# Where weights and activations stand modulo 512 bytes: a decoder block on one core

## The chip, the core and the metric

The kernel runs on one core of one Trainium2 chip. The time is the device time of one execution in microseconds (us). TensorE is called PE, its weight loads PEld, VectorE DVE, ScalarE ACT, GpSimd POOL, and the queue that issues the DMAs of weights SP. SBUF is the on-chip memory: 128 partitions, in each of which a tile takes the same range of bytes. "The place" of a tile is the byte in the partition at which it begins, taken modulo 512.

## The reference, cut to what matters

One decoder layer on x of 256 tokens by 2048 channels, in float32:

```python
proj = x @ w_in                         # q, k, v, gates of two mixers, merge gates
o_gla = gated_linear_attention(...) ; o_fox = forgetting_attention(...)
merged = sigmoid(ma) * (o_gla @ w_branch_gla) + sigmoid(mb) * (o_fox @ w_branch_fox)
x = layer_norm(ALPHA * x + merged @ w_out)
h = gelu(causal_dwconv(x @ w_gate)) * (x @ w_up)
x = layer_norm(ALPHA * x + h @ w_down)
x = x + sigmoid(x @ w_ple_gate) * (p @ w_ple_proj)
```

Nearly all of the arithmetic is in the products with weight matrices.

## The kernel before, in words

A product of float32 numbers is made of three products of a shorter format (float32r). Each operand is split into `hi`, its rounded value, and `lo`, the rest: a product is hi·hi + lo·hi + hi·lo, all summed in PSUM. ACT makes `hi` from a raw row (`copy`, line 101), DVE makes `lo` = raw - hi (line 127). Activations are kept split in tiles `xT`, `oT`, `mT`, `x1T`, `hT`, `x2T`: per 128 channels 256 numbers of hi tokens and 256 of lo tokens.

The weights come from HBM in 284 units (`wu`), each of two halves of 128x1024 numbers. `prep` (lines 116 to 130) loads a half into a `raw` tile (4 of them), and ACT and DVE make a `hi` and a `lo` tile of it (6 each). `unit` gives out units in order, up to three ahead. A matmul has two operands in SBUF: the stationary one, 128 columns which PEld loads into the array, and the moving one, which streams through it. There are two kinds of stages:

- **Weights stationary** (`w_unit`, lines 190 and 192; `w_phase`, lines 203 and 207). For each 128x128 block of weights: the hi weights are loaded and 512 columns of activations (hi and lo tokens) stream, then the lo weights are loaded and 256 columns (hi tokens) stream. These are the projections fq, fk, gq, gk (`psfq`, `psfk`, `psq`, `psk`), the merge gates (`psm`), the branches (`psa`, `psb`), and gate and up of the MLP (`psg`, `psu`). `w_phase` makes the first three units of the MLP in two halves of the tokens, each matmul with 256 columns: first all hi weights for one half (line 203), then hi and lo weights in turn (lines 203 and 207).
- **Activations stationary** (`x_mm`, line 234). For each block of 128 tokens, hi tokens are loaded and hi weights stream (512 columns, two banks `c`), then hi tokens and lo weights, then lo tokens and hi weights. These are `gv`, `gr`, `wo`, `dn`, `pg`, and the small projection `pp`, whose weights `pw` are tiles of their own. The first stage, `fv` (line 341), does the same with tiles of 1048 columns in three chunks (`fch`).

The order of the instructions of each engine comes from a list scheduler that works by the program's order and given priorities; SP's DMAs stand in program order. The mixers' small work is pulled in between by generators.

Pools are laid one behind another in SBUF, so the size of each pool sets the places of all behind it. Two pools hold nothing but a gap: `gap0` (64 bytes) between the hi and the lo tiles, and `gap1` (448 bytes) behind the lo tiles. The places (modulo 512 bytes) that come of it:

| tiles | before | after the change |
|---|---|---|
| hi weights, in weights-stationary units | 0 | 64 |
| hi weights, in activations-stationary units | 0 | 0 |
| lo weights | 64 | 0 |
| activations, `pw`, `fvhi`, `fvlo` (pool `big`) | 0 | 0 |
| chunks of `fv` within their tiles | 0, 384, 256 | 0, 0, 0 |
| raw rows of weights (4 tiles) | 0, 96, 192, 288 | 0 |
| `t1`, `t2` (small tiles of mixers and evacuations) | 384 | 0 |
| `hT10` (last hidden block of the MLP) | 128 | 0 |

Within these tiles blocks begin at whole multiples of 512 bytes, so a block's place is that of its tile.

Of the kernel before, what the change touches and what calls it, by code (L numbers as in the profile page):

```python
# [9 lines left out]
F32 = mybir.dt.float32  # L10
F32R = mybir.dt.float32r
# [8 lines left out]
P = 128  # L20
# [6 lines left out]
FH = 8  # L27
# [5 lines left out]
NS = 1048  # L33
# [4 lines left out]
AFF_DVE = (0, 2)  # L38
LN_ORDER = (1, 0, 3, 2)
GROWS = 96  # L40
PAD = 88
S8W = 2048

OFF = dict(gq=0, gk=1024, gv=2048, gr=4096, glr=6144, fq=6160, fk=7184, fv=8208,
           ff=9232, ma=9240, mb=11288)
# [3 lines left out]
def tile_block(ctx: ExitStack, tc: tile.TileContext, wu, wfv, wpp, xT_in, x_in, pT_in, wlr,  # L49
# [1 line left out]
    nc = tc.nc  # L51

    cst = ctx.enter_context(tc.tile_pool(name="cst", bufs=1))
    wide_hi = ctx.enter_context(tc.tile_pool(name="wide_hi", bufs=6))
    step = ctx.enter_context(tc.tile_pool(name="step", bufs=1))
    gap0 = step.tile([P, 16], F32, name="gap0")
    wide_lo = ctx.enter_context(tc.tile_pool(name="wide_lo", bufs=6))
    step2 = ctx.enter_context(tc.tile_pool(name="step2", bufs=1))
    gap1 = step2.tile([P, 112], F32, name="gap1")
    big = ctx.enter_context(tc.tile_pool(name="big", bufs=15))  # L60
    ring = ctx.enter_context(tc.tile_pool(name="ring", bufs=4))
    sm = ctx.enter_context(tc.tile_pool(name="sm", bufs=2))
# [6 lines left out]
    chn = cst.tile([P, chan.shape[1]], F32, name="chn")  # L69
    ident = cst.tile([P, P], F32, name="ident")  # L70
    mhalf = cst.tile([P, 1], F32, name="mhalf")
    pad = cst.tile([P, PAD], F32, name="pad")

    def s8(shape, dt=F32, name=None):
        t = big.tile([P, S8W], dt, tag="S8", name=name)
        n = int(np.prod(shape[1:]))
        t = t[:shape[0], :n]
        if len(shape) == 3:
            return t.rearrange("p (a b) -> p a b", b=shape[2])
        if len(shape) == 4:  # L80
            return t.rearrange("p (a b c) -> p a b c", b=shape[2], c=shape[3])
        return t

    def w_tile(tag, dt, name):
        pool = wide_hi if tag == "hi" else wide_lo
        return pool.tile([P, 1024], dt, tag=tag, name=name)

    def t1(name):
        return sm.tile([P, 256], F32, tag="t1", bufs=6, name=name)

    def t2(name):
        return sm.tile([P, 512], F32, tag="t2", bufs=6, name=name)

    def mmtile(name):
        return pmm.tile([P, 512], F32, tag="mm", name=name)
# [4 lines left out]
    def copy(o, i, scale=1.0):  # L100
        nc.scalar.activation(o, i, AF.Copy, bias=0.0, scale=scale)  # L101
# [15 lines left out]
    def prep():  # L117
        u = n_prep[0]
        n_prep[0] += 1
        his, los = [], []  # L120
        for h in range(2):
            raw = ring.tile([P, 1024], F32, tag="raw", bufs=4, name=f"raw{u}_{h}")
            nc.sync.dma_start(raw, wu[u, :, h * 1024:(h + 1) * 1024])
            hi = w_tile("hi", F32R, f"hi{u}_{h}")
            copy(hi, raw)
            lo = w_tile("lo", F32R, f"lo{u}_{h}")
            nc.vector.tensor_tensor(lo, raw, hi.bitcast(F32), ALU.subtract)  # L127
            his.append(hi)
            los.append(lo)
        ready[u] = (his, los)  # L130
# [4 lines left out]
    def unit():  # L135
        u = n_used[0]
        n_used[0] += 1
        while n_prep[0] < min(NU, u + 3):
            prep()
        return ready.pop(u)  # L140
# [161 lines left out]


    fv = s8([P, 2, 1024], name="fv")
    fch = ((0, 352), (352, 352), (704, 344))
    fbk = [[mmtile(f"fv_{t}{c}") for c in range(3)] for t in range(2)]

    def fv_prep(u, hs=(0, 1), his=None, los=None):
        his, los = his or [], los or []
        for h in hs:  # L310
            raw = ring.tile([P, NS], F32, tag="raw", bufs=4, name=f"fvraw{u}_{h}")
            hi = s8([P, NS], F32R, name=f"fvhi{u}_{h}")
            lo = s8([P, NS], F32R, name=f"fvlo{u}_{h}")
            for o, n in fch if u == 0 else ((0, NS),):
                e = slice(o, o + n)
                nc.sync.dma_start(raw[:, e], wfv[u, :, h, e])
                copy(hi[:, e], raw[:, e])
                nc.vector.tensor_tensor(lo[:, e], raw[:, e], hi[:, e].bitcast(F32), ALU.subtract)
            his.append(hi)
            los.append(lo)  # L320
        return his, los

    load_x(0, 0, 1, 1)
    f0 = fv_prep(0, (0,))
    load_x(0, 1, 2, 1)
    fvu = [fv_prep(0, (1,), *f0)]
    load_x(0, 2, 4)
    fvu.append(fv_prep(1))
    load_x(1, 0, 4)
    for u in range(8):  # L330
        hi, lo = fvu[u]
        for j in range(2):
            kt = 2 * u + j
            a = xT[kt // 4][:, kt % 4, :]
            for cs in ((0,), (1,), (2,)) if u == 0 else ((0, 1, 2),):
                for t in range(2):
                    ah, al = a[:, t * P:t * P + P], a[:, 256 + t * P:256 + t * P + P]
                    for i, (w, x) in enumerate(((hi[j], ah), (lo[j], ah), (hi[j], al))):
                        for c in cs:
                            o, n = fch[c]  # L340
# [20 lines left out]
    for t in range(2):  # L361
        tk = t1("smtok")
        nc.gpsimd.memset(tk, 0.0)
        for i in range(3):
            copy(tk[:, 32 * i:32 * i + 16], fbk[t][2][:, 320:336])
        copy(tk[:, P:P + FH], fbk[t][2][:, 336:344])
        nc.tensor.transpose(smp[:GROWS, t * P:t * P + P], tk[:, 0:GROWS], ident)
        nc.tensor.transpose(smp[:FH, 256 + t * P:256 + t * P + P], tk[:, P:P + FH], ident)
    for t in range(2):
# [147 lines left out]
    for nm, dst, sc in (("fq", fq, P ** -0.5), ("fk", fk, 1.0)):  # L517
        if nm == "fk":
            mixers.append(fox_gen())
        for n in range(8):  # L520
            hi, lo = unit()
# [8 lines left out]
    for nm, dst, sc in (("q", gq, 1.0 / 16.0), ("k", gk, 1.0)):  # L530
        for n in range(8):
            hi, lo = unit()
            ps = mmtile(f"ps{nm}{n}")
            w_unit(ps, hi, lo, xT, range(16), True, True)
            h, c = n // 2, n % 2
# [163 lines left out]
    for n in range(32):  # L699
        hi, lo = unit()  # L700
# [7 lines left out]
        pull(1)  # L708
    early.close()
    late = ctx.enter_context(tc.tile_pool(name="late", bufs=1))  # L710


    mT = [s8([P, 4, 512], F32R, name=f"mT{i}") for i in range(4)]
    fhl = None
    for n in range(16):
        hi, lo = unit()
# [162 lines left out]
        return banks  # L879

    z1 = [s8([P, 2048], name=f"z1{t}") for t in range(2)]
    st1 = [sm.tile([P, 4, 6], F32, tag=f"st1{t}", bufs=1, name=f"st1{t}") for t in range(2)]
    gain = [None, None]

    def mid1():
# [82 lines left out]
    tc.keep_in_program_order(nc.scalar.preload_act_table_set("gelu_apprx_tanh_and_others"))  # L968


    gp = [late.tile([P, 264], F32, name=f"gp{i}") for i in range(2)]
    for i in range(2):
        nc.gpsimd.memset(gp[i][:, 0:2], 0.0)
    hT = [None] * 11
# [12 lines left out]
    for n in range(NF):  # L987
# [17 lines left out]
        u = t1("up")  # L1005
# [6 lines left out]
            pull(1)  # L1012

    z2 = [s8([P, 2048], name=f"z2{t}") for t in range(2)]
    st2 = [sm.tile([P, 4, 6], F32, tag=f"st2{t}", bufs=1, name=f"st2{t}") for t in range(2)]

    def mid2():
        for t in range(2):
# [127 lines left out]
```

## Time and profile before

| what | value |
|---|---|
| median of 3 runs | 1701.79 us (1701.62 to 1701.97) |
| the profiled execution, its own time | 1702.23 us |
| its span, first to last instruction | 1699.5 us |
| granted clock of TensorE | 1.0 |
| PE busy, PEld busy | 99%, 86% of the span |
| DVE, ACT, POOL busy | 65%, 49%, 2% |
| matmuls | 9035 |

What lies around the span is 2.7 us. A matmul's busy time in the profile runs from its first column to a modelled end, and matmuls overlap; so a busy PE says nothing of how fast it goes. What one matmul costs is the time from its start to the next one's start. Where matmuls of one kind follow each other, the mean duration of a row less the overlap with the next gives the same thing.

### The profile page before, as it was taken

The numbers are of one execution on the slowest core, as the hardware profiler recorded it, in microseconds if no ns is written. First come the engines' busy times: TensorE is split into PE (matmuls) and PEld (weight loads), VectorE is DVE, ScalarE is ACT, GpSimd is POOL, SyncE is SP. The second block draws the span as 40 slices with busy tenths as digits, with TensorE's granted clock in tenths as the row PEclk, the third lists the DMA queues.
The fourth block names the chain that finished last, engine by engine and source line by source line (L and its number), as shares of the span: only waits on it lengthen the run. The fifth ranks groups of instructions, "written<-read, shape, count | busy, mean of one in ns | idle before, by whom it ended". The sixth has DMA issues, their size and how long they took to land.

```text
span 1699.5 us, 23843 instructions
## 1 busy us (share of the span) xinstructions
PE 1690.2 (99%) x9035; PEld 1456.4 (86%) x9035; DVE 1098.0 (65%) x1588; ACT 833.9 (49%) x1200; POOL 36.7 (2%) x123
## 2 busy tenths in 40 slices
PE   9999999999999999999999999999999999999998
PEld 8888888888888888888888888888888888888787
DVE  6666658758756547774687776666666644544774
ACT  5655545445555544443365445445445433334633
POOL 0100000000000000000010000000000000000000
PEclk9999999999999999999999999999999999999999
DMA  7765555555555556557656665555555575566455
GB/s 266 260 198 166 165 185 180 178 175 178 181 174 173 162 187 192 190 189 281 220 165 197 215 215 191 192 190 188 188 195 188 191 287 189 187 194 199 158 175 172
DMA packets 91427, 330.22 MB, mean 194 GB/s; under 512 B 10232, under 2 KB 11904, under 8 KB 89904
## 3 DMA queue, kind: packets, MB, share of 16 engines
q1 hardware_dynamic: 90528, 324.51, 58.8%
q0 software_dynamic: 784, 4.20, 0.7%
q8 instruction: 70, 1.15, 0.3%
q14 instruction: 45, 0.37, 0.1%
HBM read 323.42 MB, written 5.25 MB: 193 GB/s over the span
## 4 chain that ended last, share of the span: by engine, by line
PE 98%; DVE 1%; ACT 0%; DMA 0%; SPq 0%; issue 0%; POOL 0%; ACTq 0%
PE dn L234 14%; PE psu L190 9%; PE psg L190 9%; PE psm L190 7%; PE gv L234 5%; PE gr L234 5%; PE pg L234 5%; PE wo L234 5%; PE psu L192 5%; PE psg L192 5%; PE psm L192 4%; PE psa L190 3%; PE fv L341 2%; PE psa L192 2%; PE psq L190 2%; PE psfk L190 2%
## 5 line engine op out<-in xcount | busy, mean ns | idle before, releaser
L127 DVE TENSOR_TENSOR lo<-raw,hi 128x1024 fp32r<-128x1024 f32 x568 | 694.2, 1224 | 506.9 <-ACT hi L101 505.7
L101 ACT ACTIVATE hi<-raw 128x1024 fp32r<-128x1024 f32 x568 | 601.7, 1060 | 732.6 <-issue 274.7
L190 PE MATMUL psu<-x1T,hi 128*128 128x512 f32 x688 | 240.4, 392 | 0.0
L190 PE MATMUL psg<-x1T,hi 128*128 128x512 f32 x672 | 234.8, 392 | 0.0
L192 PE MATMUL psu<-x1T,lo 128*128 128x256 f32 x688 | 192.3, 280 | 0.0
L234 PE MATMUL dn<-hi,hT 128*128 128x512 f32 x704 | 192.1, 392 | 0.0
L192 PE MATMUL psg<-x1T,lo 128*128 128x256 f32 x672 | 187.8, 280 | 0.0
L190 PE MATMUL psm<-xT,hi 128*128 128x512 f32 x512 | 179.8, 395 | 0.0
L234 PEld LDWEIGHTS dn<-hi,hT 128*128 128x128 f32 x704 | 132.1, 188 | 30.6
L190 PEld LDWEIGHTS psu<-x1T,hi 128*128 128x128 f32 x688 | 129.2, 188 | 27.6
L190 PEld LDWEIGHTS psg<-x1T,hi 128*128 128x128 f32 x672 | 126.2, 188 | 27.0
L192 PE MATMUL psm<-xT,lo 128*128 128x256 f32 x512 | 143.2, 280 | 0.0
L192 PEld LDWEIGHTS psu<-x1T,lo 128*128 128x128 f32 x688 | 130.6, 190 | 0.0
L192 PEld LDWEIGHTS psg<-x1T,lo 128*128 128x128 f32 x672 | 127.6, 190 | 0.0
L190 PEld LDWEIGHTS psm<-xT,hi 128*128 128x128 f32 x512 | 96.2, 188 | 21.2
L234 PE MATMUL dn<-lo,hT 128*128 128x512 f32 x352 | 111.9, 395 | 0.0
L192 PEld LDWEIGHTS psm<-xT,lo 128*128 128x128 f32 x512 | 97.0, 189 | 0.2
L190 PE MATMUL psa<-oT,hi 128*128 128x512 f32 x256 | 89.5, 392 | 0.0
L234 PEld LDWEIGHTS dn<-lo,hT 128*128 128x128 f32 x352 | 66.1, 188 | 14.8
L234 PE MATMUL gv<-hi,xT 128*128 128x512 f32 x256 | 72.6, 395 | 0.0
L234 PE MATMUL gr<-hi,xT 128*128 128x512 f32 x256 | 72.4, 395 | 0.0
L192 PE MATMUL psa<-oT,lo 128*128 128x256 f32 x256 | 71.6, 280 | 0.0
(247 smaller groups left out, 2435.2 us busy)
## 6 DMA issues: line engine op xcount, KB each, us to landing
raw<-in_wu_dram SPq DMA_DIRECT2D x568, 512.0 KB, 4.6
fvraw<-in_wfv_dram SPq DMA_DIRECT2D x14, 524.0 KB, 6.5
lnb<-in_lng_dram SPq DMA_DIRECT2D x4, 1024.0 KB, 13.3
z<-in_x_dram SPq DMA_DIRECT2D x2, 1024.0 KB, 9.5
praw<-in_wpp_dram SPq DMA_DIRECT2D x4, 512.0 KB, 4.5
x1d<-z POOLq DMA_DIRECT2D x2, 1024.0 KB, 7.6
z<-x1d SPq DMA_DIRECT2D x2, 1024.0 KB, 9.6
xraw<-in_xT_dram SPq DMA_DIRECT2D x7, 256.0 KB, 7.1
```

Of the source, the lines that this page charges most:

```text
L101: nc.scalar.activation(o, i, AF.Copy, bias=0.0, scale=scale)
L127: nc.vector.tensor_tensor(lo, raw, hi.bitcast(F32), ALU.subtract)
L190: nc.tensor.matmul(ps, lhsT=hi[i // 8 if hoff == 0 else 0][:, w0 % 1024:w0 % 1024 + P], rhs=a[:, kt % 4, :], start=first and i == 0, stop= ...
L192: nc.tensor.matmul(ps[:, 256:512], lhsT=lo[i // 8 if hoff == 0 else 0][:, w0 % 1024:w0 % 1024 + P], rhs=a[:, kt % 4, 0:256], start=False, ...
L234: nc.tensor.matmul(bs[j][:, 0:m], lhsT=x, rhs=v[:, o:o + m], start=first and i == 0, stop=last and i == 2)
L341: nc.tensor.matmul(fbk[t][c][:, 0:n], lhsT=x, rhs=w[:, o:o + n], start=kt == 0 and i == 0, stop=kt == 15 and i == 2)
```

## The change

The hi and lo tiles come out of one pool `wide`. A hi tile is 1152 numbers wide instead of 1024, and its 1024 numbers are put 16 numbers (64 bytes) into it in units whose weights are stationary, and at its beginning in the units of `XSTAT` (gv, gr, wo, dn, pg). The lo tiles, and with them all pools behind, come to 0 modulo 512 bytes. The raw rows of the first stage, 1048 numbers wide, are taken from the six hi tiles instead of the four raw tiles, which so shrink to 1024 numbers. The chunks of `fv` are 384, 384 and 280 columns instead of 352, 352 and 344. `gp`, the two buffers of the MLP's convolution, are two of the six `t2` tiles instead of tiles of the pool `late`; some small statistics tiles (`st1`, `st2`) and paddings are moved so that the places come out even.

```diff
-    wide_hi = ctx.enter_context(tc.tile_pool(name="wide_hi", bufs=6))
-    step = ctx.enter_context(tc.tile_pool(name="step", bufs=1))
-    gap0 = step.tile([P, 16], F32, name="gap0")
-    wide_lo = ctx.enter_context(tc.tile_pool(name="wide_lo", bufs=6))
-    step2 = ctx.enter_context(tc.tile_pool(name="step2", bufs=1))
-    gap1 = step2.tile([P, 112], F32, name="gap1")
+    wide = ctx.enter_context(tc.tile_pool(name="wide", bufs=6))
...
-    def w_tile(tag, dt, name):
-        pool = wide_hi if tag == "hi" else wide_lo
-        return pool.tile([P, 1024], dt, tag=tag, name=name)
+    def w_tile(tag, dt, name, u):
+        if tag == "lo":
+            return wide.tile([P, 1024], dt, tag=tag, name=name)
+        o = 0 if u in XSTAT else HSTEP
+        return wide.tile([P, WH], dt, tag=tag, name=name)[:, o:o + 1024]
...
-    fch = ((0, 352), (352, 352), (704, 344))
+    fch = ((0, 384), (384, 384), (768, 280))
...
-            raw = ring.tile([P, NS], F32, tag="raw", bufs=4, name=f"fvraw{u}_{h}")
+            raw = wide.tile([P, WH], F32, tag="hi", name=f"fvraw{u}_{h}")[:, 0:NS]
...
-    gp = [late.tile([P, 264], F32, name=f"gp{i}") for i in range(2)]
+    gp = [t2(f"gp{i}")[:, 0:264] for i in range(2)]
```

with `XSTAT = (*range(32, 64), *range(120, 136), *range(224, 284))`, `WH = 1152` and `HSTEP = 16`.

The order of PE, DVE, ACT and SP stays what it was, but for the widths in the first stage. On PE, in the steady part of that stage, one block of tokens before (`fv_126` to `fv_131` are its six banks, `fvhi` and `fvlo` the weights, `xT` the tokens):

```order
L341 MATMUL fv_126<-fvhi_0_169,xT_111 128x352
L341 MATMUL fv_127<-fvhi_0_169,xT_111 128x352
L341 MATMUL fv_128<-fvhi_0_169,xT_111 128x344
L341 MATMUL fv_129<-fvhi_0_169,xT_111 128x352
L341 MATMUL fv_130<-fvhi_0_169,xT_111 128x352
L341 MATMUL fv_131<-fvhi_0_169,xT_111 128x344
```

and the same place in the changed program (the numbers of the buffers differ, the banks are the same six):

```order
L344 MATMUL fv_118<-fvhi_0_161,xT_103 128x384
L344 MATMUL fv_119<-fvhi_0_161,xT_103 128x384
L344 MATMUL fv_120<-fvhi_0_161,xT_103 128x280
L344 MATMUL fv_121<-fvhi_0_161,xT_103 128x384
L344 MATMUL fv_122<-fvhi_0_161,xT_103 128x384
L344 MATMUL fv_123<-fvhi_0_161,xT_103 128x280
```

The same matmuls stand in the same order, with the 1048 columns cut elsewhere.

On POOL the two memsets of the borders of `gp` move. Before, they stand ahead of the mixers' second half (`gst`), as soon as the pool `late` is open:

```order
L549 MEMSET at 128x1536
L973 MEMSET gp_8157 128x2
L973 MEMSET gp_8158 128x2
L664 ISA
L664 TENSOR_TENSOR gst<-gst,mhalf 128x1 x8
L786 TENSOR_TENSOR mv<-mv,mhalf 128x1 x2
L910 DMA ppd<-ppo 128x512 x4
L995 COPY gp_8157<-gp_8157 128x1 x2
L995 COPY gp_8158<-gp_8158 128x1 x2
```

In the changed program they stand behind the four DMAs that write `ppo` out, since `gp` now takes `t2` tiles that such work held:

```order
L552 MEMSET at 128x1536
L667 ISA
L667 TENSOR_TENSOR gst<-gst,mhalf 128x1 x8
L790 TENSOR_TENSOR mv<-mv,mhalf 128x1 x2
L913 DMA ppd<-ppo 128x512 x4
L976 MEMSET gp_8148 128x2
L976 MEMSET gp_8149 128x2
L998 COPY gp_8148<-gp_8148 128x1 x2
L998 COPY gp_8149<-gp_8149 128x1 x2
```

The memsets now come right before the first use of `gp` (the copies), 15 instructions later in POOL's order than before.

More of the change, by code (lines that the diff above doesn't have):

```diff
@@ L40 @@
 GROWS = 96
-PAD = 88
+PAD = 16
+LPAD = 24
+XSTAT = (*range(32, 64), *range(120, 136), *range(224, 284))
 S8W = 2048
+WH = 1152
+HSTEP = 16
 OFF = dict(gq=0, gk=1024, gv=2048, gr=4096, glr=6144, fq=6160, fk=7184, fv=8208,
@@ L71, in tile_block @@
     mhalf = cst.tile([P, 1], F32, name="mhalf")
+    st1 = [cst.tile([P, 4, 6], F32, name=f"st1{t}") for t in range(2)]
+    st20 = cst.tile([P, 4, 6], F32, name="st20")
     pad = cst.tile([P, PAD], F32, name="pad")
@@ L123, in prep @@
             nc.sync.dma_start(raw, wu[u, :, h * 1024:(h + 1) * 1024])
-            hi = w_tile("hi", F32R, f"hi{u}_{h}")
+            hi = w_tile("hi", F32R, f"hi{u}_{h}", u)
             copy(hi, raw)
-            lo = w_tile("lo", F32R, f"lo{u}_{h}")
+            lo = w_tile("lo", F32R, f"lo{u}_{h}", u)
             nc.vector.tensor_tensor(lo, raw, hi.bitcast(F32), ALU.subtract)
@@ L364, in tile_block @@
         for i in range(3):
-            copy(tk[:, 32 * i:32 * i + 16], fbk[t][2][:, 320:336])
-        copy(tk[:, P:P + FH], fbk[t][2][:, 336:344])
+            copy(tk[:, 32 * i:32 * i + 16], fbk[t][2][:, 256:272])
+        copy(tk[:, P:P + FH], fbk[t][2][:, 272:280])
         nc.tensor.transpose(smp[:GROWS, t * P:t * P + P], tk[:, 0:GROWS], ident)
@@ L710, in tile_block @@
     late = ctx.enter_context(tc.tile_pool(name="late", bufs=1))
+    late.tile([P, LPAD], F32, name="lpad")
     mT = [s8([P, 4, 512], F32R, name=f"mT{i}") for i in range(4)]
@@ L881, in tile_block @@
     z1 = [s8([P, 2048], name=f"z1{t}") for t in range(2)]
-    st1 = [sm.tile([P, 4, 6], F32, tag=f"st1{t}", bufs=1, name=f"st1{t}") for t in range(2)]
     gain = [None, None]
@@ L1014, in tile_block @@
     z2 = [s8([P, 2048], name=f"z2{t}") for t in range(2)]
-    st2 = [sm.tile([P, 4, 6], F32, tag=f"st2{t}", bufs=1, name=f"st2{t}") for t in range(2)]
+    st2 = [st20, sm.tile([P, 4, 6], F32, tag="st2", bufs=1, name="st21")]
     def mid2():
```

## The prediction

> **What bounds the kernel now.** I read the page first, then totals by line, the timeline of a steady stretch, groups of instructions in narrow windows, and the chain by stage. The page:
>
> ```profile
> span 1699.5 us, 23843 instructions
> PE 1690.2 (99%) x9035; PEld 1456.4 (86%) x9035; DVE 1098.0 (65%) x1588; ACT 833.9 (49%) x1200; POOL 36.7 (2%) x123
> PE 98%; DVE 1%; ACT 0%; DMA 0%; SPq 0%; issue 0%; POOL 0%; ACTq 0%
> ```
>
> The last row is the chain that ended last: PE holds 98% of it, and DVE, ACT and the DMAs have slack. So only what changes the rhythm of the matmuls can move the time by much. The change removes no matmul and no column. It moves bytes. The question is whether a matmul's cost hangs on the places of its two operands. Two windows over the whole span, of lines 190 and 234 alone, give the counts:
>
> ```profile
> 0.00:1699.50 1699.50, 965.42 (x2768) 519.82 (x2768) 1.00 0.60 194
> 0.00:1699.50 1699.50, 620.22 (x2688) 494.77 (x2688) 1.00 0.60 194
> ```
>
> There are 2768 pairs with stationary weights (each hi matmul of line 190 is followed by a lo one of line 192) and 2688 matmuls with stationary activations. The timeline of a steady piece of the first kind:
>
> ```profile
> 613.28 0.28 PE L192 MATMUL psm<-xT,lo 128*128 128x256 f32 x1
> 613.28 0.19 PEld L190 LDWEIGHTS psm<-xT,hi 128*128 128x128 f32 x1
> 613.39 0.39 PE L190 MATMUL psm<-xT,hi 128*128 128x512 f32 x1
> 613.40 0.19 PEld L192 LDWEIGHTS psm<-xT,lo 128*128 128x128 f32 x1
> 613.62 0.28 PE L192 MATMUL psm<-xT,lo 128*128 128x256 f32 x1
> 613.74 0.39 PE L190 MATMUL psm<-xT,hi 128*128 128x512 f32 x1
> ```
>
> Each load starts with a matmul and fetches the weights of the next one: the lo weights come in while the 512 columns stream, the hi weights while the 256 stream. So two reads of SBUF run side by side, and the pair that matters is (moving tile, next stationary tile). Start to start a hi matmul takes 0.23 us, a lo one 0.12; the recorded duration is about 162 ns more, which turns means of groups into costs. Means, from 600 to 630 us and from 524 to 534:
>
> ```profile
> L190 PE MATMUL psm<-xT,hi 128*128 128x512 f32 x87 | 30.2, 392 | 0.0
> L192 PE MATMUL psm<-xT,lo 128*128 128x256 f32 x88 | 24.6, 279 | 0.0
> ...
> L190 PE MATMUL psm<-xT,hi 128*128 128x512 f32 x30 | 10.6, 398 | 0.0
> L192 PE MATMUL psm<-xT,lo 128*128 128x256 f32 x29 | 8.1, 280 | 0.0
> ```
>
> The usual pair is 230 + 117 = 347 ns. In the second window the same pair, at the same places, takes 236 + 117 = 353. So there is more than one steady rhythm, and places alone don't settle which.
>
> With stationary activations, `dn` from 1360 to 1458 us (its first half) and from 1480 to 1582 (its second):
>
> ```profile
> L234 PE MATMUL dn<-hi,hT 128*128 128x512 f32 x284 | 77.4, 394 | 0.0
> L234 PE MATMUL dn<-lo,hT 128*128 128x512 f32 x141 | 44.1, 393 | 0.0
> ...
> L234 PE MATMUL dn<-hi,hT 128*128 128x512 f32 x297 | 79.6, 389 | 0.0
> L234 PE MATMUL dn<-lo,hT 128*128 128x512 f32 x148 | 46.9, 397 | 0.0
> ```
>
> Two rhythms again: about 232 ns for all, or 227 where hi weights (place 0) stream and 235 where lo weights (place 64) stream, both over activations at 0. In the second the place shows: 64 bytes apart cost 8 ns.
>
> **Stationary activations, part by part.** After the change both weights stream from place 0. The trace holds such a stage: `pp`, whose `pw` and `pTs` are all at 0. From 856.6 to 858.3 us, and just after a start, 1598 to 1599.9:
>
> ```profile
> L234 PE MATMUL pp<-pw,pTs 128*128 128x512 f32 x9 | 2.2, 389 | 0.0
> L234 PE MATMUL pp<-pw,pTs 128*128 128x512 f32 x7 | 1.8, 394 | 0.0
> ```
>
> Settled, nine in a row cost 389 - 162 = 227 each; unsettled, 232. The stages now, from the chain (start, us, matmuls; `gv` and `gr` in runs of 24 between pulls):
>
> ```profile
> 259.94 5.53 PE gv L234 x24
> ...
> 764.01 83.45 PE wo L234 x360
> 1352.24 238.32 PE dn L234 x1032
> 1609.84 42.52 PE pg L234 x184
> ```
>
> That is 230.4, 231.8, 230.9 and 231.1 ns each. At 227 the 1056 of `dn` save 3.9 x 1056 = 4.1 us, the 384 of `wo` 1.8, some 336 of `pg` 1.4. In `gv` and `gr` a small product interrupts every 24; I count half of each run as unsettled (a mean of 229): 1.4 x 768 = 1.0 us. Sum: -8.3 us. Bounds: all 768 settled too, -9.9; nothing ever settled, at 232, +2.8 (1.2 + 0.1 + 0.3 + 1.2).
>
> **Stationary weights.** The window of the hi matmul (512 columns) now sees lo weights loaded from 64, after the change from 0. That is the case of 512 columns with both at 0: 227 by the `pp` row, against 230. The window of the lo matmul (256 columns) now sees hi weights from 0, afterwards from 64. The nearest rows are in `w_phase`, whose matmuls are 256 columns: first hi after hi, all at 0; then hi and lo in turn, so that every second load comes from 64.
>
> ```profile
> 864.14 2.16 PE L203 MATMUL psu<-x1T,hi 128*128 128x256 f32 x16
> 872.33 0.28 PE L207 MATMUL psg<-x1T,lo 128*128 128x256 f32 x1
> 875.13 0.28 PE L207 MATMUL psg<-x1T,lo 128*128 128x256 f32 x1
> ```
>
> All at 0: 2.16 less the last one's 0.28 and less 0.09 that the first loses behind transposes (872.12 to 872.33 is 0.21 there instead of 0.12) is 1.79 us for 15, or 119 ns. In turn: 24 starts in 2.80 us, or 117. So a load from 64 costs a window of 256 columns nothing, and 117 is my value. Pair: 227 + 117 = 344, 3 ns less, x 2768 = -8.3 us.
>
> ```profile
> 872.12 0.37 PE L203 MATMUL psg<-x1T,hi 128*128 128x256 f32 x1
> ```
>
> Bounds: alternating took about 3 ns off each matmul against all at 0 (227 + 120 = 347), which twice is 341, -6 x 2768 = -16.6 us; the 353 ns rhythm is +16.6 us. I take the middle value since it is nearest to rows with the same widths in each window.
>
> The Trainium skill (TensorE: Matmul & The Clock Gate, LDWEIGHTS) gives the load of 128 columns as columns / 1.2, or 107 ns. By that, an estimate, the 256-column window is bound by its load and has at most 10 ns in it at any place; the trace's 117 agrees.
>
> **The rest.** Raw rows at other places cost ACT and DVE nothing: over four raw places line 127 has
>
> ```profile
> L127 DVE TENSOR_TENSOR lo<-raw,hi x568: 1187/1225/1230, 55.0 to 1680.8; 128x1024 fp32r<-128x1024 f32 x190
> ```
>
> (minimum, median, maximum in ns), no spread to win. First stage: 1048 columns and 288 matmuls stay; 3 ns either way is ±0.9 us, taken 0. Its first chunk grows by 32 columns, under 0.3 us in DMA, ACT and DVE; PE later waits anyway for a DMA issued at 4.96 and for ACT, and from 13.47 runs through, so six raw places instead of four find no wait to remove:
>
> ```profile
> 4.96 6.07 DMA fvraw<-in_wfv_dram
> 11.05 1.09 ACT fvhi L101
> 13.47 37.38 PE fv L341 x235
> ```
>
> On SP the order stays; its `fvraw` issues wait for one of six hi tiles instead of one of four raw tiles, so for older work than before, and the units' loads queued behind them come no later. The memsets of `gp` go behind the DMAs of `ppo` on POOL, and the copies of `gp` behind them:
>
> ```profile
> 862.60 1.07 POOL L910 DMA_DIRECT2D ppd<-ppo  x2 [2.57 <-ACT ppo L101]
> 881.55 0.31 POOL L995 COPY gp<-gp 128x1 f32<-128x1 f32 x2 [17.89 <-DVE gp L217]
> ```
>
> From 863.7 to 881.5 POOL is idle; the `ppo` tile has to land in that time. 18 us cover it. Without that cover PSUM banks would come free late and PE would wait.
>
> Sum: the execution's own 1702.23 - 8.3 - 8.3 = 1685.6. The median of the runs shown is 0.4 lower, so 1685.2.
>
> **Rivals.** (1) *The pair stays.* 227 + 120, the sum with all at 0, is the same 347 as now, so the loss may belong to the pair and only move from one window to the other. For it: the two windows were never seen apart with these widths. Then 1701.8 - 8.3 = 1693.5. (2) *The pair falls into the 353 ns rhythm*, the rival that ends slower. Place: lines 190 and 192; a start behind other work decides the rhythm, and the trace has that of 353 from 524 to 534 us with no change of places, so it is stable once entered. Price 353 - 347 = 6 x 2768 = 16.6 us, against 8.3 gained: 1701.8 + 8.3 = 1710.1. It decides from 350 ns a pair (3 x 2768 = 8.3 us eats the gain). Against it: from 900 to 1300 us, the longest stretch, every group is at 392,
>
> ```profile
> L190 PE MATMUL psg<-x1T,hi 128*128 128x512 f32 x579 | 202.4, 392 | 0.0
> L190 PE MATMUL psu<-x1T,hi 128*128 128x512 f32 x576 | 201.3, 392 | 0.0
> ```
>
> so the 353 rhythm is the rarer one, at the old places. (3) *Activations never settle* at all-0, as in the row of seven: -8.3 + 2.8, 1696.3. (4) *Places don't matter*, the change does nothing for PE: 1701.8. For it: two speeds at equal places; against: 389 against 397 in `dn`. The Trainium skill (SBUF — State Buffer, Who interferes with whom) has this rule: TensorE's reads of moving and of stationary data go through independent ports, and PE never waits on anyone. By that rule all of the sum above is zero; the 389 and 397 of one stage speak against it.
>
> **The numbers.** Forecast 46%, with its own range 1676 to 1691 (the low bounds together; either gain only a third of what I count); (1) 20%, (2) 17%, (3) 8%, (4) 7%, 2% for what I don't see. Low end: both lower bounds, 1701.8 - 16.6 - 9.9 = 1675.3, so 1676. High end: leaving (2) mostly out, 1705, which takes in (4) and a pair at 350 ns with half of the other gain. Of no change this kernel's runs can tell 0.2%, 3.4 us. Faster: forecast, (1), (3) less tails, 0.73. Within: (4) and tails, 0.08. Slower: (2) and tails, 0.19.
>
> **What would show it.** Right: `dn` and `wo` hi and lo rows both at 389; `psu` and `psg` at 389 with lo at 279 or 280. Wrong in (1): hi rows 392, lo rows 279, or 389 and 283. In (2): a sum of durations of the pair of 678, as at 524 us, in most units. In (3): `dn` rows at 394. If a wait of PE shows at 880 us, `gp` was not covered. The forecast is wrong if the weights-stationary stages grow, whatever `dn` does.

## The result and the profile after

The changed kernel takes 1700.85 us (median of 12 runs, 1698.69 to 1703.09), beside 1703.74 for the kernel before (12 runs, 1701.62 to 1707.01): a ratio of 0.9985, interval [0.9976, 0.9994]. It is faster by some 3 us; 16.6 were forecast. The profiled execution took 1700.97 us, against 1702.23 before.

Page, the span, the busy times and the chain that ended last by engine:

```profile
span 1699.0 us, 23839 instructions
PE 1688.3 (99%) x9035; PEld 1458.9 (86%) x9035; DVE 1098.0 (65%) x1588; ACT 834.1 (49%) x1200; POOL 37.8 (2%) x123
PE 96%; DMA 1%; DVE 1%; ACT 1%; SPq 0%; issue 0%; POOL 0%; ACTq 0%
```

PE still carries the chain, so the answer is again in the rhythm of its matmuls. In the durations of the groups, 389, 392, 394 and 397 ns stand for 227, 230, 232 and 235 ns from start to start, and a pair's cost is the sum of its two durations less some 325 ns.

**Activations stationary.** Pieces of the chain (start, us, matmuls), and `dn` in its second half:

```profile
268.88 5.46 PE gv L237 x24
...
765.14 19.12 PE wo L237 x84
...
1357.04 234.00 PE dn L237 x1032
1610.32 41.65 PE pg L237 x184
```

```profile
L237 PE MATMUL dn<-hi,hT 128*128 128x512 f32 x295 | 78.9, 389 | 0.0
L237 PE MATMUL dn<-lo,hT 128*128 128x512 f32 x148 | 45.5, 389 | 0.0
```

Hi and lo weights now both cost 227 ns, where lo weights cost 235. `dn` went from 238.32 to 234.00 us for the same 1032 matmuls, a run of 24 in `gv` from 5.53 to 5.46, `pg` from 42.52 to 41.65 for 184, and `wo` from 231.8 to 227.6 ns each in the piece shown.

**Weights stationary.** Groups from 900 to 1300 us (gate and up of the MLP), then from 600 to 630 and from 524 to 534 us (merge gates):

```profile
L193 PE MATMUL psu<-x1T,hi 128*128 128x512 f32 x574 | 202.5, 394 | 0.0
L193 PE MATMUL psg<-x1T,hi 128*128 128x512 f32 x570 | 201.1, 394 | 0.0
L195 PE MATMUL psu<-x1T,lo 128*128 128x256 f32 x573 | 161.0, 281 | 0.0
L195 PE MATMUL psg<-x1T,lo 128*128 128x256 f32 x570 | 160.2, 281 | 0.0
...
L193 PE MATMUL psm<-xT,hi 128*128 128x512 f32 x87 | 30.5, 394 | 0.0
L195 PE MATMUL psm<-xT,lo 128*128 128x256 f32 x86 | 24.2, 281 | 0.0
...
L193 PE MATMUL psm<-xT,hi 128*128 128x512 f32 x30 | 10.3, 389 | 0.0
L195 PE MATMUL psm<-xT,lo 128*128 128x256 f32 x30 | 8.3, 276 | 0.0
```

The hi rows went from 392 to 394, and the pair from 347 to 350 ns. In six stretches of `psm`, one of them at 524 us, the pair takes 389 + 276 - 325 = 340 instead, at the same places. Start-to-start times summed over all pairs of a stage, in us:

| stage | before | after | lo at 64 | hi at 192 |
|---|---|---|---|---|
| `psfq`, `psfk`, `psq`, `psk` (511 pairs) | 179.9 | 183.1 | 179.9 | 179.9 |
| `psm` (512) | 179.2 | 178.1 | 178.3 | 175.2 |
| `psa`, `psb` (384) | 133.1 | 134.4 | 133.1 | 130.6 |
| `psu`, `psg` (1360) | 471.5 | 476.0 | 471.5 | 462.4 |
| sum | 963.7 | 971.6 | 962.8 | 948.1 |

(The last two columns are experiments below.) Start-to-start times summed in the same way over the stages with stationary activations fell by 4.4 us in `dn`, 2.2 in `gv` and `gr`, 1.1 in `pg` and 0.9 in `wo`, 8.5 in all, and the pairs took 7.9 back. In `wo` the faster matmuls alone are worth 1.7 us, but three starts in a row came 0.9 us late in sum, behind DVE additions that have to read a bank out:

```profile
810.31 1.10 PE L237 MATMUL wo<-hi,mT 128*128 128x512 f32 x2 [0.22 <-DVE z L838]
```

The row covers two matmuls, each behind a short wait. The chain goes back from there over DVE and ACT to a raw row of weights that landed only at 807.2 us. Together the stages give -0.6; the spans differ by 0.5.

**A stretch at half clock.** 1.6 of the 7.9 us are not a matter of places. Timeline of PE after the first stage, and granted clock (PEclk, third number from the end) from 56 to 58 and 58 to 60 us:

```profile
56.42 0.59 PE L193 MATMUL psfq<-xT,hi 128*128 128x512 f32 x1
56.81 0.42 PE L195 MATMUL psfq<-xT,lo 128*128 128x256 f32 x1
57.02 0.63 PE L193 MATMUL psfq<-xT,hi 128*128 128x512 f32 x1
```

```profile
56.00:58.00 2.00, 1.80 (x6) 1.62 (x7) 2.00 (x3) 2.00 (x6) 0.00 (x0) 0.61 0.34 100
58.00:60.00 2.00, 2.00 (x8) 1.67 (x7) 1.97 (x4) 1.97 (x4) 0.00 (x0) 0.54 0.89 274
```

Between 53 and 56 us PE is busy for only 1.6 us of 3, before the change and after. In this execution six pairs behind that gap were slow, four of them at 640 to 644 ns and the ones at the ends at 601 and 492; in the profiled execution of before none was. The execution in the column "hi at 192" has four pairs of 640 ns too. The Trainium skill (TensorE: Matmul & The Clock Gate, What's actually happening) says that the gate halves the clock after an idle window, and that the windows run free of the kernel; that the same gap brings half clock in some executions and not in others agrees.

### The profile page after: what moved, and what is told of

It is laid out like the page before. It is cut to its first block, busy times and chain, and to the rows that moved or that the text cites. A ratio compares the mean times of both kernels' runs of the same rounds, so it can differ in the third digit from the quotient of the medians.

```text
span 1699.0 us, 23839 instructions
## 1 busy us (share of the span) xinstructions
PE 1688.3 (99%) x9035; PEld 1458.9 (86%) x9035; DVE 1098.0 (65%) x1588; ACT 834.1 (49%) x1200; POOL 37.8 (2%) x123
## 4 chain that ended last, share of the span: by engine, by line
PE 96%; DMA 1%; DVE 1%; ACT 1%; SPq 0%; issue 0%; POOL 0%; ACTq 0%
PE dn L237 14%; PE psu L193 9%; PE psg L193 9%; PE psm L193 7%; PE gv L237 5%; PE gr L237 5%; PE psu L195 5%; PE pg L237 5%; PE psg L195 5%; PE psm L195 4%; PE psa L193 3%; PE wo L237 3%; PE fv L344 2%; PE psfq L193 2%; PE psa L195 2%; PE psk L193 2%
## 5 line engine op out<-in xcount | busy, mean ns | idle before, releaser
L195 PEld LDWEIGHTS psu<-x1T,lo 128*128 128x128 f32 x688 | 130.6, 190 | 0.0
```

Of the source, the lines that this page charges most:

```text
L195: nc.tensor.matmul(ps[:, 256:512], lhsT=lo[i // 8 if hoff == 0 else 0][:, w0 % 1024:w0 % 1024 + P], rhs=a[:, kt % 4, 0:256], start=False, ...
```

## The experiments

The failed term is the pair with stationary weights: 350 ns where 344 was forecast. Two theories:

- **A, windows.** Each window, moving tile and tile loaded meanwhile, has a cost of its own set by the two places. The forecast rests on it.
- **B, rhythms.** A stream of pairs falls into one of a few steady rhythms. Places decide which of them can be entered, and the start decides which one is entered; no window has a cost of its own.

**All tiles at 0.**

```diff
-HSTEP = 16
+HSTEP = 0
```

> The changed kernel with hi weights at 0 everywhere (all places 0 modulo 512 bytes). Theory A (each window of a pair has a cost of its own, set by the places of its moving tile and of the tile loaded meanwhile): 512 columns with both at 0 cost 227 ns, 256 columns 120, so a pair is 347 in every stage; about 8 us less than the changed kernel. Theory B (the pair has a few steady rhythms, and places and the start choose among them; no window has a cost of its own): the pair may settle at any of 340, 347, 350 or 353, with more than one of them in one run; the stages with stationary activations stay at 227 under both theories.

1704.82 us (one run), 4 us more than the changed kernel, where theory A gave 8 less. From 1200 to 1250 us:

```profile
L193 PE MATMUL psu<-x1T,hi 128*128 128x512 f32 x72 | 25.7, 399 | 0.0
L195 PE MATMUL psu<-x1T,lo 128*128 128x256 f32 x72 | 20.2, 281 | 0.0
```

The pair is 399 + 281 - 325 = 355 by these rows, and by single starts a cycle of 350, 361 and 349 ns, 353.3 in the mean. By windows it should have been 227 + 120 = 347, since both sizes had been seen with all at 0. They had been seen in streams of equal widths. The hi window takes 237 here, not 227: a window's cost cannot be carried from one stream to another. And this is not what these places always give. In `psa` and `psb` of the same run, from 640 to 760 us, the places are also all 0, and by single starts the pair takes 346.7 ns:

```profile
L193 PE MATMUL psa<-oT,hi 128*128 128x512 f32 x236 | 82.5, 391 | 0.0
L195 PE MATMUL psa<-oT,lo 128*128 128x256 f32 x235 | 65.8, 280 | 0.0
```

That is the sum that theory A gave, but not its parts: 230 + 117, where they should have been 227 + 120. `psm` has both rhythms.

**The other half alone: lo at 64, hi at 0 where weights are stationary.** Everything else of the change stays; now the lo tiles are the wide ones.

```diff
     def w_tile(tag, dt, name, u):
-        if tag == "lo":
+        if tag == "hi":
             return wide.tile([P, 1024], dt, tag=tag, name=name)
...
-            raw = wide.tile([P, WH], F32, tag="hi", name=f"fvraw{u}_{h}")[:, 0:NS]
+            raw = wide.tile([P, WH], F32, tag="lo", name=f"fvraw{u}_{h}")[:, 0:NS]
```

> The two halves of the change apart: where weights are stationary hi at 0 and lo at 64, as before the change; where activations are stationary both at 0, as after it. Theory A and B: pairs at 347 (230 + 117) as before, dn and wo at 227 as after. Against the kernel before -8 us (ratio about 0.995), against the changed kernel -8 us. If instead the pairs come out at 350, what slows them in the changed kernel isn't the place of hi and lo but something else that moved with them (raw rows, small tiles, DVE and ACT).

1693.21 us (5 runs, 1692.19 to 1694.37), ratio to before 0.9938 [0.9924, 0.9951]. From 900 to 1300 us, and `dn` in the chain:

```profile
L193 PE MATMUL psg<-x1T,hi 128*128 128x512 f32 x576 | 201.3, 392 | 0.0
L195 PE MATMUL psg<-x1T,lo 128*128 128x256 f32 x576 | 161.0, 280 | 0.0
...
1348.15 233.98 PE dn L237 x1032
```

The pairs are back at 346.7 ns, with the sum of before to 0.1 us in `psu` and `psg`, and `dn` keeps its 234. This is the activations' half by itself: -10.5 us by the medians, where -8 was expected, and -9.0 by the profiled spans. 0.9 of it comes from `psm`, where four stretches took 353 ns before and none does here, at the same places. The pairs' half costs the rest, 7.6 us by the medians. Pool order, first stage and `gp` cost nothing that shows.

**Where the hi tile stands, in one kernel.** MLP units 136 to 223 take 22 hi places, four units each; lo and activations at 0.

```diff
+OFFS = (0, 64, 4, 72, 8, 80, 12, 88, 16, 96, 20, 104, 24, 112, 28, 120, 32, 116, 40, 124, 48, 56)
...
-        o = 0 if u in XSTAT else HSTEP
+        o = 0 if u in XSTAT else OFFS[(u - 136) // 4] if 136 <= u < 224 else HSTEP
```

> The changed kernel, but in the gate and up projections of the MLP the place of hi is changed every four units through 22 values from 0 to 496 bytes, lo at 0. Theory A: the cost of the 256-column window alone changes with the place, the 512-column window stays at one value; equal cost on both sides of a change of block. Theory B: both windows change together, the sum takes only a few values some 3.3 ns apart (340 to 353), and the first pairs of a block still carry the rhythm of the block before. 64 bytes again at 350, if the place decides; at 340 or 350, if the start does.

1698.65 us (one run). The two blocks that matter, 64 bytes (1048.4 to 1059.3 us) and 192 bytes (1316.4 to 1326.9):

```profile
L194 PE MATMUL psg<-x1T,hi 128*128 128x512 f32 x16 | 5.7, 396 | 0.0
L196 PE MATMUL psg<-x1T,lo 128*128 128x256 f32 x16 | 4.5, 281 | 0.0
...
L194 PE MATMUL psg<-x1T,hi 128*128 128x512 f32 x16 | 5.5, 389 | 0.0
L196 PE MATMUL psg<-x1T,lo 128*128 128x256 f32 x16 | 4.4, 276 | 0.0
```

Places of 0, 256 and 64 gave 353 ns, 128 and 384 gave 352; 96, 480, 464 and 160 gave 346.7; 224 gave 344; 192 gave 340.0 (226 + 114); the others 349 to 351. So theory B's "only a few values some 3.3 ns apart" does not hold as it stands, since there are steady means between. A block took up its rhythm within the first few pairs. Two things follow. Only the loads in the lo window changed place, but most of the change is in the hi window, 226 to 237 ns; the lo window stayed between 114 and 120. So the cost of a window hangs on more than its own two places, which theory A doesn't allow. And 64 bytes gave 353 ns here and 350 in the changed kernel.

**Where the lo tile stands.** The same list for lo, hi at 0.

```diff
-        if tag == "lo":
+        if tag == "hi":
             return wide.tile([P, 1024], dt, tag=tag, name=name)
-        o = 0 if u in XSTAT else HSTEP
+        o = 0 if u in XSTAT else OFFS[(u - 136) // 4] if 136 <= u < 224 else HSTEP
...
-            raw = wide.tile([P, WH], F32, tag="hi", name=f"fvraw{u}_{h}")[:, 0:NS]
+            raw = wide.tile([P, WH], F32, tag="lo", name=f"fvraw{u}_{h}")[:, 0:NS]
```

> As the scan of hi, but hi stays at 0 and the place of lo goes through the same 22 values. Theory A: the 512-column window alone changes: 230 at 64 bytes, 227 at 0. Theory B: both windows change together; 64 bytes again at 347 in sum. Places that give 340 or less steadily would be candidates for a faster kernel.

1695.61 us (one run). 13 of 22 places gave 346.7 ns, among them the old 64; none less. The worst were 0, 256, 480 and 224, with 353; at 224 (1333.4 to 1344 us):

```profile
L194 PE MATMUL psg<-x1T,hi 128*128 128x512 f32 x15 | 5.3, 395 | 0.0
L196 PE MATMUL psg<-x1T,lo 128*128 128x256 f32 x14 | 3.9, 282 | 0.0
```

For lo, too, both windows change: hi between 229 and 237 ns, lo between 113 and 120. The kernel before stood at one of the many places that give the usual rhythm here.

**hi at 192 throughout.**

```diff
-HSTEP = 16
+HSTEP = 48
```

> hi at 192 bytes instead of 64 wherever weights are stationary, lo at 0, activations-stationary units unchanged. In the scan of hi places the four units at 192 ran at 340.0 ns a pair (226 + 114). Places decide: all 2768 pairs at 340, that is 6.7 ns under the kernel before each, -18.5 us, with the -10.5 us that the activations-stationary half is worth: about 1675 us. Starts decide: a good part of the stages stays at 346.7 or 350 and the time lies between 1680 and 1701.

1677.66 us (5 runs, 1676.86 to 1678.41), ratio 0.985 [0.9837, 0.9864]: 25.7 us under the kernel before. From 900 to 1300 us:

```profile
L193 PE MATMUL psg<-x1T,hi 128*128 128x512 f32 x589 | 202.1, 389 | 0.0
L195 PE MATMUL psg<-x1T,lo 128*128 128x256 f32 x589 | 162.6, 276 | 0.0
```

All 1360 pairs of the MLP and the 384 of `psa` and `psb` take 340.0 ns, and in `psm` all but some 50 of 512. In the first four stages only half do, some 260 of 511; 204 run at 350 or a little more, at the same places. The time lies between what the two theories gave: 3 us above 1675, and under 1680.

**Does the start decide?** Blocks of 64 and 192 bytes behind different neighbours.

```diff
+OFFS = (48, 16, 0, 16, 48, 16, 120, 16, 64, 16, 48, 40, 48, 0, 48, 120, 48, 8, 48, 56, 48, 16)
...
-        o = 0 if u in XSTAT else HSTEP
+        o = OFFS[(u - 136) // 4] if 136 <= u < 224 else 0 if u in XSTAT else HSTEP
```

> One kernel in which the MLP units 136 to 223 take the hi places 192, 64, 0, 64, 192, 64, 480, 64, 256, 64, 192, 160, 192, 0, 192, 480, 192, 32, 192, 224, 192, 64 bytes in turn, four units each, lo at 0. Places decide: every block of 64 shows one and the same pair sum, and so does every block of 192 (340). Starts decide (the rhythm is inherited from the block ahead): blocks of 64 differ, 340 behind 192 and 350 or 353 behind 0, 256 and 480; blocks of 192 differ likewise.

1696.49 us (one run). The block at 64 behind 192 (890 to 902 us), behind 0 (936 to 946.9) and behind 480 (1025.5 to 1036.5):

```profile
L194 PE MATMUL psg<-x1T,hi 128*128 128x512 f32 x21 | 7.2, 389 | 0.0
L196 PE MATMUL psg<-x1T,lo 128*128 128x256 f32 x20 | 5.5, 276 | 0.0
...
L194 PE MATMUL psg<-x1T,hi 128*128 128x512 f32 x16 | 5.6, 394 | 0.0
L196 PE MATMUL psg<-x1T,lo 128*128 128x256 f32 x16 | 4.5, 281 | 0.0
...
L194 PE MATMUL psg<-x1T,hi 128*128 128x512 f32 x16 | 5.7, 396 | 0.0
L196 PE MATMUL psg<-x1T,lo 128*128 128x256 f32 x16 | 4.5, 281 | 0.0
```

The same places, three rhythms: 340.0, 350.0 and 353.3 ns, each steady for all 64 pairs of its block. In this kernel 64 took 340 only behind a block of 192 that ran at 340; behind 192 at 350 it took 350. 192 took 340 behind 64 at 353, behind 160, 480 and 224, and 350 behind 0, 32 and 64 at 350. That is theory B, with one correction: a block need not go on in the rhythm of the block ahead. 64 took 350 behind 0 at 353, and 353 behind 480 at 347.

**Places close around 192**, most 4 bytes apart.

```diff
+OFFS = (36, 38, 40, 42, 43, 44, 45, 46, 47, 48, 49, 50, 51, 52, 54, 56, 58, 60, 62, 16, 17, 18)
...
-        o = 0 if u in XSTAT else HSTEP
+        o = OFFS[(u - 136) // 4] if 136 <= u < 224 else 0 if u in XSTAT else HSTEP
```

> The same scan with hi places close around 192 bytes: 144 to 248, most in steps of 4, and then 64, 68, 72. If a hit of moving and loaded rows in the same 64-byte piece is what costs, the sum changes in steps at 128, 192 and 256 only; if the distance in bytes counts, it changes gradually and has a lowest place, expected at 192 with 340.0 and 344 to 350 on both sides. Nothing under 340 is expected.

1699.11 us (one run). 340.0 came at 168, 192 and 204 (and at 64, entered from 248 here), and next to them 172 gave 353, 188 350, 196 and 200 346.7. Blocks at 168 (938.5 to 949 us) and 172 (960.5 to 971):

```profile
L194 PE MATMUL psg<-x1T,hi 128*128 128x512 f32 x16 | 5.5, 389 | 0.0
L196 PE MATMUL psg<-x1T,lo 128*128 128x256 f32 x16 | 4.4, 276 | 0.0
...
L194 PE MATMUL psg<-x1T,hi 128*128 128x512 f32 x15 | 5.3, 397 | 0.0
L196 PE MATMUL psg<-x1T,lo 128*128 128x256 f32 x15 | 4.2, 280 | 0.0
```

Neither of the two patterns expected shows: there is no step at whole 64 bytes and no valley around 192. From 168 to 172, four bytes further, the pair goes from 340 to 353 ns. Each place stands here behind one neighbour only, so which of these values a place can have in another order is not shown.

**Where streaming weights stand.** Units 224 to 283 (`dn` and `pg`), 15 hi places; lo and activations at 0.

```diff
-        o = 0 if u in XSTAT else HSTEP
+        o = OFFS[(u - 224) // 4] if 224 <= u < 284 else 0 if u in XSTAT else HSTEP
```

> The scan with stationary activations: hi places in the units 224 to 283 (dn), four units each, 0, 256, 32, 288, 64, 320, 96, 352, 128, 384, 160, 416, 192, 448, 224 bytes; lo and the activations at 0. Here hi weights stream, and activations are loaded meanwhile. Own cost of a window by its two places: hi windows run from 227 at 0 to about 235 elsewhere (lo weights at 64 took 235 in the kernel before), and 192 may again be lower, at or under 226. Rhythms: steps of 3.3 ns, with none below 226.

1705.42 us (one run). Places 0 and 256 (1357 to 1397 us), then 32 (1400 to 1421):

```profile
L238 PE MATMUL dn<-hi,hT 128*128 128x512 f32 x120 | 32.1, 389 | 0.0
L238 PE MATMUL dn<-lo,hT 128*128 128x512 f32 x59 | 18.3, 389 | 0.0
...
L238 PE MATMUL dn<-hi,hT 128*128 128x512 f32 x61 | 16.6, 393 | 0.0
L238 PE MATMUL dn<-lo,hT 128*128 128x512 f32 x32 | 10.0, 395 | 0.0
```

At the eleven places from 32 to 192 in the list's order a block's mean lies between 231 and 232 ns, 192 among them, and the lo weights, whose own place stayed at 0, slow down with the hi weights. The last two, 448 and 224, fell into the end of `pg`, whose short runs say nothing of a steady rate. So the activations' half of the change stood at the best of the places tried, and with stationary activations, too, a window's cost depends on more than its own two places.

**One block at the head decides for the rest.** The changed kernel with units 136 to 139 alone at 192, and the kernel with 192 throughout with those units alone at 0.

```diff
-        o = 0 if u in XSTAT else HSTEP
+        o = 0 if u in XSTAT else 48 if 136 <= u < 140 else HSTEP    # first kernel, HSTEP = 16
+        o = 0 if u in XSTAT else 0 if 136 <= u < 140 else HSTEP     # second kernel, HSTEP = 48
```

> The changed kernel (hi at 64), but the first four MLP units, 136 to 139, have hi at 192; the other 84 MLP units stay at 64. Starts decide: the 340 ns rhythm of the units at 192 is inherited, as it was at unit 140 of the run with mixed places, and all of the MLP runs at 340 instead of 350: some 1330 pairs x 10 ns, -13.3 us against the changed kernel, about 1687.5 us. Places decide: the 84 units at 64 stay at 350 and the time stays at about 1700.5.

> The reverse: hi at 192 throughout, but at 0 in the units 136 to 139. Starts decide: behind units at 0, units at 192 ran at 350 before, so the whole MLP does: +13.3 us against the kernel with 192 everywhere, about 1691. Places decide: the 84 units at 192 stay at 340, and the time at about 1678.

1686.99 us (4 runs, 1686.53 to 1688.6; ratio 0.9906 [0.9891, 0.9921]) and 1691.42 (4 runs, 1690.26 to 1692.17; 0.993 [0.9915, 0.9944]). From 900 to 1300 us, behind the block that differs, in the first and in the second:

```profile
L193 PE MATMUL psg<-x1T,hi 128*128 128x512 f32 x586 | 201.1, 389 | 0.0
L195 PE MATMUL psg<-x1T,lo 128*128 128x256 f32 x585 | 161.5, 276 | 0.0
...
L193 PE MATMUL psg<-x1T,hi 128*128 128x512 f32 x570 | 201.1, 395 | 0.0
L195 PE MATMUL psg<-x1T,lo 128*128 128x256 f32 x571 | 160.2, 280 | 0.0
```

This settles it. With 84 of 88 MLP units at the places of the changed kernel, the MLP runs at 340 instead of 350; with 84 of 88 at 192 it runs at 350 instead of 340. Since `w_phase` makes the units 136 to 138, unit 139 with its 16 pairs is the only one at the other place in the mixed stream. In the first kernel it ran at 340, in the second at 353, and the units behind it at 350. Each time the rhythm that was taken up behind the head was kept to the end, some 450 us later, and the times came within 0.6 us of what theory B gave.

**Other places for the first four stages**, where 192 catches 340 only half the time: 204 and 168.

```diff
-        o = 0 if u in XSTAT else HSTEP
+        o = 0 if u in XSTAT else 51 if u < 32 else HSTEP    # 42 in the second kernel
```

> hi at 192, but at 204 in the first 32 units (psfq, psfk, psq, psk), where with 192 some 180 of 511 pairs ran at 350 instead of 340. In the fine scan 204 gave 340.0 as well. If 204 finds 340 behind the stops of these stages, -1.8 us, about 1676; if it falls elsewhere in part of them, up to +3 us, 1681.

> The same with 168 in the first 32 units, the third place that gave 340.0: again -1.8 us if it finds that rhythm behind the stops, up to +3 us if it falls elsewhere. A place with no other stable rhythm would show 340 in all of psfq, psfk, psq and psk.

1677.30 us (4 runs, 1675.54 to 1677.71; ratio 0.9845 [0.9831, 0.986]) and 1679.59 (1678.77 to 1679.87; 0.9859 [0.9843, 0.9876]). `psfq` and `psq` from 60 to 250 us, with 204 and with 168:

```profile
L193 PE MATMUL psq<-xT,hi 128*128 128x512 f32 x128 | 45.9, 402 | 0.0
L193 PE MATMUL psfq<-xT,hi 128*128 128x512 f32 x123 | 42.3, 391 | 0.0
...
L193 PE MATMUL psq<-xT,hi 128*128 128x512 f32 x128 | 45.4, 399 | 0.0
L193 PE MATMUL psfq<-xT,hi 128*128 128x512 f32 x122 | 43.8, 401 | 0.0
```

These means mix rhythms and stops. By single starts each place finds 340 behind some stops and a slower rhythm behind others, 353 with 204 and up to 355.6 with 168. With 204 the time is that of 192, with 168 it is 2 us more. No place was found that has only the 340 rhythm. The kernels with 192, and with 204 in the first four stages, are the fastest here.

## Why the prediction was wrong, step by step

- **Right in the main: PE's rhythm is what counts.** The two halves of the change add up: by the profiled spans the activations' half is worth -8.1 us without what `psm` gave there, and the pairs' half +7.9, which makes -0.2 against -0.5. The slack of DVE, ACT and the DMAs did not hold everywhere: with the faster matmuls `wo` ran into late weights, which cost 0.9 us.
- **Right: activations stationary, -8.3 us.** It measured -8.5 by the sums over the stages. The mechanism came as forecast, a rate of 227 for hi and lo; that the sum is so near is in part luck, since its misses cancel. `dn` gave 4.4 us instead of 4.1; `gv` and `gr` settled sooner than counted and gave 2.2, not 1.0; `pg` gave 1.1 instead of 1.4, and `wo` 0.9 instead of 1.8, for the wait just named. Rival (3) did not come.
- **Wrong: weights stationary, 227 + 117 = 344 ns.** The pair took 350 in most of the kernel, 3.3 ns more instead of 3 less: +7.9 us, 1.6 of them from the stretch at half clock, where -8.3 stood. The step that failed is not one of the two sizes but the addition: 227 came from a stream in which all matmuls have 512 columns, 117 from one in which all have 256. With all at 0, where both were known, the mixed pair of the MLP gave 353 (236.7 + 116.7) and that of `psa` and `psb` 346.7 (230 + 116.7), at the same places modulo 512, and never 227 + 120; and moving only what the lo window loads changed the hi window by 11 ns. What the runs showed in its place is a rhythm of the whole stream, chosen by start and places: with 84 of 88 MLP units unmoved, the four at the head took the rest from 350 to 340 ns.
- **The rivals.** (1), the pair stays at 347, and (2), the pair falls to 353, both missed; 350 is between them, at just the point named as the one that eats the gain. (2) had the mechanism: "a start behind other work decides the rhythm", "stable once entered". That had been read from one window of the trace and then priced as the rarer case of a cost that places set. A stage with two rhythms at equal places should have weighed against any price per place. The range, 1676 to 1705, reached that far for this reason.
- **Rival (4), places don't matter,** fell in every scan. That its 1701.8 us is within 1 us of the measured time is chance: a gain of 8.5 us and a loss of 7.9 nearly cancel. The Trainium skill (SBUF — State Buffer, Who interferes with whom) says that moving and stationary reads go by independent ports and PE waits on no one; the same matmuls at 340.0 to 356.6 ns a pair, with nothing but a tile's place changed, do not agree with a reading of that rule by which place is free.
- **Right: the rest.** No wait of PE stands at 880 us where `gp` could have been late, and the first stage's `fv` took 37.38 us for its 235 matmuls before and after.

What in the chip makes a stream lock into a rhythm, and why 168, 192 and 204 can hold 340, stays open; the runs show only that start and places together choose. That places repeat after 512 bytes was assumed throughout and not tested.

## What to carry to other kernels

When the same instructions at the same addresses show two steady speeds in one trace, a change of address cannot be priced from single windows of other streams: measure the very sequence, with its widths. A scan inside one kernel, a few units for each place, is cheap for finding the rates, but a block's rhythm depends on its neighbour, so the place found has to be run throughout. And look at the head of a long stream: four units there were worth some 14 us.

## What the runs showed of the hardware

- Alternating matmuls of 512 and 256 columns, each with a load of 128 columns, ran most often at steady pair times of 340.0, 346.7, 350.0 and 353.3 ns, and kept one of them over more than a thousand pairs. Some blocks of the scans ran steadily at other values, such as 344.5, 352.0 and 356.6.
- Four bytes of a tile's place went with 13 ns of a pair (168 to 172 bytes, in one order). When the hi weights moved, whose load falls into the lo window, most of the change was in the hi window (226 to 237 ns against 114 to 120).
- For streams of 512 columns alone the best places of the moving hi weights were 0 and 256 bytes, with lo weights and activations at 0: 227 ns against 231 to 232 at eleven others.
- After a gap in which PE was partly idle for 3 us, some of the profiled executions ran the next 3 us or so at half clock (granted 0.54, pairs of 640 ns), others did not.
